# A two-layer decoder step on one core: samples' products, scores and weighted values placed anew, and accumulators that are not zeroed

## The chip, the cores and the metric

One NeuronCore of a Trainium2 chip. The metric is the device time of one execution in microseconds. Engines are named as in the profile: PE is TensorE's matmuls (PEld its weight loads), DVE VectorE, ACT ScalarE, POOL GpSimd, SP the engine that issues most of the DMAs.

## The reference

One inference step of a decoder trunk with two layers of model width 1024, for a prompt of 1024 tokens and 8 samples of one token each, which share all weights:

```python
def a_mixer(hn, w_in, lb, hg_gain, mem_k, mem_v, w_o, s0):     # layer 0
    q_h, f_h, i_h, g_h, q_m = jnp.split(hn @ w_in, 5, axis=-1)
    ...
    o, S = hgrn2_scan(q, k, v, logf, s0)       # S = f*S + k v ; o = q S, per head 128x128
    o = rmsnorm(o.astype(hn.dtype), hg_gain) * jax.nn.silu(g_h).reshape(...)
    om = mem_attend(q_m.reshape(B, L, MEM_HEADS, MEM_DH), mem_k, mem_v)
    out = jnp.concatenate([o.reshape(B, L, MIX_HALF), om.reshape(B, L, MIX_HALF)], axis=-1) @ w_o

def b_mixer(hn, w_in, bias, k_all, v_all, q_pos, k_pos, mem_k, mem_v, w_o):   # layer 1
    q_s, q_m = jnp.split(hn @ w_in, 2, axis=-1)
    os_ = stick_breaking(...)                  # over the shared K/V, with a running sum of log(1-p)
    om = mem_attend(...)                       # 4 heads over 256 memory tokens

# every layer: h = h + rmsnorm(mix); h = h + rmsnorm(swiglu(rmsnorm(h)))
```

For each sample the memory attention and the stick-breaking attention run over that sample's own cache: 256 keys and values of 4 heads x 128.

## The kernel before, in words

The 1024 prompt tokens are two groups, g = 0 and g = 1, of 512; the 8 samples ride with group 1, which is then 520 wide. Every weight product keeps float32 accuracy by splitting both operands into a high and a low part in the matmul's reduced format, and takes three matmuls. A weight piece of 512 x 128 is loaded by SP into `wraw` (5 buffers); ACT casts it to the high part (L217, or L611 for the gate products) into `ws` (5 buffers), and DVE subtracts to get the low part (L218, L613). `split[0]` always names the last of these subtractions. Activations are split alike (L238, L239).

A part of a layer is a generator that yields after each piece of work. `weave((generator, weight), ...)` draws from several of them in turn, in the ratio of their weights, and so writes one program in which the parts are interleaved; the framework's scheduler then sets the order on each engine. `tc.issue_after(ins)` ties what is issued inside it behind an instruction. The places that matter here:

- `a1` is layer 0's mixer for group 1. `a1.core` (380 to 497 us) is the prompt's recurrence. `a1.sample` (until about 550 us) is the samples' recurrence, `hgrn_sample`: for each of four heads DVE decays the state (L1329), makes the new term (L1330) from values that a DMA reads from `vd`, adds it (L1331) and multiplies with the queries (L1335). State and term are tiles of a pool `C()` of four 128x1024 buffers.
- `a1.mem` and `a1.mem_sample` (550 to 750 us) are its memory attention, for the prompt and for the samples. For a sample, `sample_scores` loads the keys into a `C()` tile and the query row `qd` (broadcast by DMA to all partitions), multiplies (L1097) and sums (L1100) on DVE. A softmax over 256 keys follows (L1169 to L1178). `sample_pv` loads the values, multiplies all of them by their probabilities (L1120, one 128x1024 product on DVE), adds the two halves of keys (L1123), splits the sum (L238, L239), and PE adds over the partitions with selector matmuls (L1111).
- `b1` is layer 1's mixer for group 1 (1500 to 1890 us): `b1.sb` (`sb_prompt`) is the prompt's stick-breaking, woven with the samples' own (`sb_sample`, its cache read by indirect DMAs on POOL) and with their memory attention, both by the two functions above. In `sb_prompt` a step makes scores (PE L1588), a bias and a cap (DVE L1599 to L1603), a softplus (ACT L1574, L1575), a running sum and a difference (DVE L1608, L1610), an exponential (ACT L1611), transposes (PE L1617, copied by ACT L1619), and the products with the values (PE L1628), which add over a head's steps in one PSUM bank. DVE sets that bank to zero first (L1625).
- Beside them run the feed-forward parts (`f0.part`, `rest()`: matmuls L231, L544, L618; ACT L261 to L263, L561; DVE L260, L264, L859), the matmuls that keep PE busy.

PSUM: `S()` has three banks, `NS()` one; the other four hold products. ACT's exponential and its sigmoid-like functions need different tables; a change of table shows as ACT_TABLE_LOAD.

Of the kernel before, what the change touches and what calls it, by code (L numbers as in the profile page):

```python
# [13 lines left out]
AF = mybir.ActivationFunctionType  # L14
ALU = mybir.AluOpType
# [8 lines left out]
def tile_decoder(  # L24
# [96 lines left out]
    def S():  # L121
        return smp.tile([P, 512], F32, tag="s", name=nm("s"))
# [39 lines left out]
    def gcol(l, i, k):  # L162
        o = (l * 4 + i) * ND + k
        return par[:, o : o + 1]
# [253 lines left out]

    def residual(g, R, rstd, gc, store, acc=None, first=False):
        n = NG[g]  # L420
        w = D // 2 if first else n
        ht = [xpool.tile([P, 2, w], F32, tag=f"x{g}", name=nm("ht")) for _ in range(ND // 2)]
        for j in range(ND // 2):
            if first:
                t0 = g * G + j * P
                nc.sync.dma_start(ht[j].rearrange("p a n -> p (a n)"), x_prompt[0, t0 : t0 + P, :])
            else:
                nc.sync.dma_start(ht[j], hs[g][:, 2 * j : 2 * j + 2, :n])
        for k in range(ND):
            if first:  # L430
                ps = NS()
                for tb in range(CH):
                    xf = ht[tb].rearrange("p a n -> p (a n)")
                    nc.tensor.transpose(ps[:, tb * P : (tb + 1) * P], xf[:, k * P : (k + 1) * P], ident)
            nc.vector.scalar_tensor_tensor(R[k][:, :n], R[k][:, :n], gc(k), rstd[:, :n], op0=ALU.mult, op1=ALU.mult)
            if first:
                nc.vector.tensor_add(R[k][:, :G], R[k][:, :G], ps)
                if g:
                    nc.vector.tensor_add(R[k][:, G:n], R[k][:, G:n], xsraw[:, k, :])
            else:  # L440
                nc.vector.tensor_add(R[k][:, :n], R[k][:, :n], ht[k // 2][:, k % 2, :])
# [16 lines left out]
    class out_proj:  # L458
# [35 lines left out]
        def finish(self):  # L494
            g, l = self.g, self.l
            rstd = rstd_from(self.acc, NG[g], 1.0 / D)
            acc = small([P, WID], tag="st", bufs=3)
            yield from residual(g, self.R, rstd, lambda k: gcol(l, 1, k), not self.last, acc, l == 0)
            r2 = rstd_from(acc, NG[g], 1.0 / D)
            yield  # L500
            yield from normed(g, self.R, r2, lambda k: gcol(l, 2, k), self.x, self.last)
# [575 lines left out]
    def sample_scores(q, load, sc):  # L1077
        qc = small([P, H * NB], tag="ss")
        for i in range(2):
            nc.vector.tensor_copy(  # L1080
                qc[:, i * 2 * NB : (i + 1) * 2 * NB].rearrange("p (h b) -> p h b", h=2), q[i][:, :, G : G + NB]
            )
        pq = S()
        for h in range(H):
# [20 lines left out]
    def sample_pv(pT, load, xo, k0):  # L1105
# [10 lines left out]
        for b in range(NB):  # L1116
            vt = load(b)
            v4 = vt.rearrange("p k (h d) -> p k h d", h=H)
            with tc.issue_after(split[0].ins):
                nc.vector.tensor_mul(v4, v4, pv4[:, :, :, b].unsqueeze(3).to_broadcast([P, 2, H, P]))  # L1120
            yield
# [10 lines left out]
        yield  # L1132
        pr = S()
        for h in range(H):
# [29 lines left out]
    def mem_attn_sample(l, qm, xo):  # L1164
# [3 lines left out]
        yield  # L1168
        pr = S()  # L1169
        for blk in range(2):  # L1170
# [8 lines left out]
        yield  # L1179
        pb = S()  # L1180
        for blk in range(2):
# [3 lines left out]
        yield  # L1185
        yield from sample_pv(pT, mem_loader(cache_mem_v, l), xo, H)

# [107 lines left out]
    def hgrn_sample(Ft, Kt, Qt, vd):  # L1295
# [25 lines left out]
        for h in range(H):  # L1321
# [6 lines left out]
            with tc.issue_after(split[0].ins):  # L1328
                nc.vector.tensor_mul(stv, stv, col(Ft))  # L1329
            nc.vector.tensor_mul(vbv, vbv, col(Kt))  # L1330
            nc.vector.tensor_add(st, st, vb)  # L1331
            nc.sync.dma_start(st_sample[0, :, h].rearrange("b k v -> k b v"), stv)
            total()
            yield
            nc.vector.tensor_mul(vbv, stv, col(Qt))  # L1335
            for a in range(2):
# [129 lines left out]
    class mixer_a:  # L1466
# [49 lines left out]
        def mem_sample(self):  # L1516
            yield from mem_attn_sample(0, self.Qm, self.xo)

# [58 lines left out]
    def sb_prompt(g, Qs, xo):  # L1577
# [44 lines left out]
        def values(h, vh, i, wt, spans):  # L1622
            if i == 0:
                po[0] = S()
                nc.vector.memset(po[0], 0.0)  # L1625
            for c, s, a, w in spans:
                for o in range(0, w, P):
                    nc.tensor.matmul(  # L1628
                        po[0][:, c * P : (c + 1) * P], vh[:, s, o : o + P], wt[:, a + o : a + o + P],
                        start=False, stop=(s == 0 and o == w - P), skip_group_check=True,  # L1630
                    )

            if i == len(units) - 1:
                put(xo, h, slice(0, G), po[0])

        po, asked, turned = [None], None, None

# [19 lines left out]
    def sb_sample(Qs, xo):  # L1657
# [7 lines left out]
        yield  # L1665
        cu = S()
        nc.tensor.matmul(cu[:, 0:HB], trif, e[:, 0:HB], start=True, stop=False)
# [7 lines left out]
    class mixer_b:  # L1675
# [33 lines left out]
        def mem_sample(self):  # L1709
            yield from mem_attn_sample(1, self.Qm, self.xo)  # L1710

# [110 lines left out]
    f0 = ffn(0, 0, o0.x)  # L1822
    weave((a1.core(), 22), (f0.part(0), 14), (islice(w0, 16), 17))
    a1.open()
    weave((a1.sample(), 12), (a1.gate(), 4), (f0.part(1), 14), (w0, 9))

# [7 lines left out]

    weave((chain(a1.merge(), a1.mem()), 27), (a1.mem_sample(), 82), (rest(), 33))
    xk0, xb0 = [], []
# [83 lines left out]
```

## Time and profile before

| | |
|---|---|
| time, three runs | 2412.99, 2409.97, 2412.3 us (median 2412.3) |
| the profiled execution | 2411.39 us, its span 2409.7 us, mean granted clock 0.998 |
| DVE products L1120, the weighted values | 24 of 1.22 us, 29.3 us |
| DVE products and sums of the samples' scores, L1097 and L1100 | 24 of 1.22 us and 24 of 1.21 us |
| DVE memsets L1625 | 8 of 0.485 us, 3.9 us |
| DMAs of the samples' memory keys | 16 of 512 KB, median 3.6 us from issue to landing |

A row of a group names the line, the engine and the operation, what is written and read, how often, and then the busy time in all, the mean of one in ns, and the idle time of the engine just before them with what ended it. A row of the waits says which engine and line waited for which, how long in all, how many times and the longest. A row of the timeline has the start, the length, the instruction and, in brackets, the idle time before it and what ended that.

### The profile page before, as it was taken

Reading aid. Unit: us, or ns where it says so; the run is one execution under the profiler, and the core shown is the slowest. Engines: PE = TensorE matmul, PEld = TensorE weight load, DVE = VectorE, ACT = ScalarE, POOL = GpSimd, SP = SyncE. Lnnn points to the kernel's source line nnn. Section 1 sums busy time; section 2 is a strip of 40 time slices with the busy share of each in tenths; the row PEclk is TensorE's granted clock in tenths of the full one; section 3 lists DMA queues with packets and bytes.
Section 4 is the critical chain, followed back from the end, with each engine's and each line's share of the span. In section 5 each row is a group of like instructions: output and inputs, shape, how many; then the busy total and the mean of one; then the engine's idle time right before and its main releaser. Section 6 shows DMA issues by size and latency. Waiting matters only on the chain.

```text
span 2409.7 us, 42324 instructions
## 1 busy us (share of the span) xinstructions
PE 2381.2 (99%) x15962; PEld 2158.6 (90%) x15962; DVE 1738.1 (72%) x3227; ACT 1275.5 (53%) x2548; POOL 113.2 (5%) x187
## 2 busy tenths in 40 slices
PE   9999999999999999999999999999999999999998
PEld 7888989888789998999999989887778899999998
DVE  5867558666896676878665777778787679676866
ACT  4547544444454554667544554556454566554445
POOL 1001202101000000000001200111000000000000
PEclk9999999999999999999999999999999999999999
DMA  6454766577644447332568846545344354343342
GB/s 195 119 169 118 171 193 167 123 191 182 200 136 141 145 144 219 115 110 81 170 177 217 229 145 189 166 140 154 113 153 122 97 158 136 105 130 100 111 127 76
DMA packets 514639, 357.59 MB, mean 148 GB/s; under 512 B 20173, under 2 KB 463674, under 8 KB 514434
## 3 DMA queue, kind: packets, MB, share of 16 engines
q1 hardware_dynamic: 498562, 312.93, 43.8%
q0 software_dynamic: 15872, 41.95, 7.4%
q8 instruction: 126, 2.06, 0.4%
q14 instruction: 79, 0.65, 0.1%
HBM read 322.86 MB, written 65.49 MB: 161 GB/s over the span
## 4 chain that ended last, share of the span: by engine, by line
PE 50%; DVE 2%; ACT 2%; issue 1%; DMA 1%; DVEq 0%; SPq 0%; ACTq 0%
PE mm L231 17%; PE q L618 16%; PE q L790 10%; PE q L544 1%; PE s L1628 1%; PE q L822 1%; PE s L1588 1%; PE s L1050 1%; PE s L1031 1%; PE s L1617 1%; DMA b<-qd 0%; DVE x L239 0%; PE ns L1111 0%; DVE ws L218 0%; PE s L1018 0%
## 5 line engine op out<-in xcount | busy, mean ns | idle before, releaser
L231 PE MATMUL mm<-x,ws 128*128 128x512 f32 (+1 forms) x5016 | 926.9, 342 | 5.5 <-DVE ws L218 2.5
L231 PEld LDWEIGHTS mm<-x,ws 128*128 128x128 f32 x5016 | 776.1, 189 | 116.0 <-DVE ws L218 3.2
L217 ACT CAST ws<-w 128x512 fp32r<-128x512 f32 x596 | 347.5, 585 | 432.6 <-PE mm L231 269.0
L218 DVE TENSOR_TENSOR ws<-w,ws 128x512 fp32r<-128x512 f32 x596 | 380.9, 645 | 227.7 <-ACT ws L217 225.1
L790 PE MATMUL q<-m,ws 128*128 128x260 f32 (+1 forms) x2496 | 304.5, 283 | 0.4
L790 PEld LDWEIGHTS q<-m,ws 128*128 128x128 f32 x2496 | 300.1, 189 | 1.6 <-ACT m L238 0.7
L618 PE MATMUL q<-y,ws 128*128 128x260 f32 (+1 forms) x1920 | 249.7, 284 | 0.2 <-ACT q L626 0.2
L618 PEld LDWEIGHTS q<-y,ws 128*128 128x128 f32 x1920 | 237.7, 189 | 1.5 <-ACT q L630 0.6
L618 PE MATMUL q<-x,ws 128*128 128x260 f32 (+1 forms) x1668 | 220.4, 283 | 3.0 <-ACT ws L611 1.6
L618 PEld LDWEIGHTS q<-x,ws 128*128 128x128 f32 x1668 | 207.9, 189 | 4.4 <-ACT ws L611 2.2
L231 PE MATMUL mm<-m,ws 128*128 128x512 f32 x768 | 187.2, 398 | 0.0
L611 ACT CAST ws<-w 128x512 fp32r<-128x512 f32 x206 | 125.1, 619 | 97.7 <-PE q L790 30.7
L613 DVE TENSOR_TENSOR ws<-w,ws 128x512 fp32r<-128x512 f32 x206 | 139.4, 688 | 45.1 <-ACT ws L611 43.0
L231 PEld LDWEIGHTS mm<-m,ws 128*128 128x128 f32 x768 | 142.7, 188 | 31.1
L799 DVE TENSOR_TENSOR r<-r,q 128x260 f32<-128x260 f32 (+1 forms) x160 | 60.6, 420 | 46.2 <-PE q L790 45.9
L544 PE MATMUL q<-x,ws 128*128 128x260 f32 (+1 forms) x720 | 87.1, 282 | 0.0
L544 PEld LDWEIGHTS q<-x,ws 128*128 128x128 f32 x720 | 86.4, 189 | 0.2
L238 ACT CAST m<-t 128x512 fp32r<-128x512 f32 (+1 forms) x88 | 54.8, 622 | 49.3 <-DVE t L859 26.7
L611 ACT CAST ws<-b 128x512 fp32r<-128x512 f32 x82 | 50.6, 620 | 38.8 <-PE q L790 13.4
L613 DVE TENSOR_TENSOR ws<-b,ws 128x512 fp32r<-128x512 f32 x82 | 56.4, 688 | 17.8 <-ACT ws L611 17.5
L239 DVE TENSOR_TENSOR m<-t,m 128x512 fp32r<-128x512 f32 (+1 forms) x88 | 60.7, 690 | 11.2 <-ACT m L238 10.4
L290 DVE TENSOR_TENSOR st<-st,n 128x512 f32<-128x512 f32 (+1 forms) x91 | 62.2, 691 | 4.2 <-ACT n L289 3.0
(422 smaller groups left out, 3092.6 us busy)
## 6 DMA issues: line engine op xcount, KB each, us to landing
w<-in_w_gu SPq DMA_DIRECT2D x275, 256.0 KB, 3.3
w<-in_w_down SPq DMA_DIRECT2D x160, 256.0 KB, 3.2
wsum<-in_w_gu POOLq DMA_DIRECT2D x48, 512.0 KB, 6.4
w<-in_w_in_a SPq DMA_DIRECT2D x80, 256.0 KB, 3.0
w<-in_w_o SPq DMA_DIRECT2D x64, 256.0 KB, 2.8
w<-wsum SPq DMA_DIRECT2D x61, 256.0 KB, 3.1
b<-in_w_gu SPq DMA_DIRECT2D x39, 256.0 KB, 4.3
b<-wsum SPq DMA_DIRECT2D x39, 256.0 KB, 3.4
```

The costliest lines, as they stand in the source:

```text
L217: nc.scalar.copy(ws[:, 0, :n, :], raw[:, :n, :])
L218: split[0] = nc.vector.tensor_sub(ws[:, 1, :n, :], raw[:, :n, :], ws[:, 0, :n, :].bitcast(F32))
L231: nc.tensor.matmul(ps[:, a, : PW[g]], wt, xt[k][:, xi, o : o + PW[g]], start=(k == 0 and wi == 0), stop=(k == nk - 1 and wi == 2),)
L238: nc.scalar.copy(dst[0], src)
L239: nc.vector.tensor_sub(dst[1], src, dst[0].bitcast(F32))
L290: nc.vector.tensor_add(acc[:, :n], acc[:, :n], t[:, :n])
L544: ins = nc.tensor.matmul(pp[a][:, :h], wt, xt[k][:, xi, a * h : (a + 1) * h], start=(k == 0 and wi == 0), stop=(k == ND - 1 and wi == 2),)
L611: nc.scalar.copy(w[:, 0, :], src)
L613: split[0] = nc.vector.tensor_sub(w[:, 1, :], src, w[:, 0, :].bitcast(F32))
L618: nc.tensor.matmul(ps[:, :h], w[:, wj, k * P : (k + 1) * P], x[:, xi, :], start=(first and k == 0 and wi == 0), stop=(k == 3 and wi == 2), ...
L790: nc.tensor.matmul(pp[a][:, :h], wt, mids[k][:, xi, a * h : (a + 1) * h], start=(k == 0 and wi == 0), stop=(k == nf - 1 and wi == 2),)
L799: nc.vector.tensor_add(d, d, pp[a][:, :h])
```

## The change

1. The samples' recurrence gets a yield between the decay and the new term, and both the new term and the product with the queries are issued behind `split[0]`.
2. The first nine steps of `a1.mem_sample` (the query rows and the scores of four samples) are woven into `a1.core`; weights of the weaves change.
3. `sb_prompt` no longer zeroes its bank: the first matmul of a head starts it, the others are tied behind that one.
4. Four transposes and a sum of the samples go from `S()` to `NS()`.
5. The residual of layer 1, group 0, is issued behind `split[0]`.
6. The samples' weighted values are made by ACT: eight copies of 128x128, each with the probability as a scale read from a pointer, in place of one DVE product.

```diff
-    def residual(g, R, rstd, gc, store, acc=None, first=False):
+    def residual(g, R, rstd, gc, store, acc=None, first=False, paced=False):
...
-            nc.vector.scalar_tensor_tensor(R[k][:, :n], R[k][:, :n], gc(k), rstd[:, :n], op0=ALU.mult, op1=ALU.mult)
+            with tc.issue_after(split[0].ins) if paced else nullcontext():
+                nc.vector.scalar_tensor_tensor(R[k][:, :n], R[k][:, :n], gc(k), rstd[:, :n], op0=ALU.mult, op1=ALU.mult)
...
-            yield from residual(g, self.R, rstd, lambda k: gcol(l, 1, k), not self.last, acc, l == 0)
+            yield from residual(g, self.R, rstd, lambda k: gcol(l, 1, k), not self.last, acc, l == 0, l == 1 and g == 0)
...
-        pq = S()
+        pq = NS()
...
-            with tc.issue_after(split[0].ins):
-                nc.vector.tensor_mul(v4, v4, pv4[:, :, :, b].unsqueeze(3).to_broadcast([P, 2, H, P]))
+            for k in range(2):
+                for h in range(H):
+                    with tc.issue_after(split[0].ins):
+                        nc.scalar.activation(v4[:, k, h, :], v4[:, k, h, :], AF.Copy, scale=pv4[:, k, h, b : b + 1])
...
-            nc.vector.tensor_mul(vbv, vbv, col(Kt))
+            yield
+            with tc.issue_after(split[0].ins):
+                nc.vector.tensor_mul(vbv, vbv, col(Kt))
...
-            nc.vector.tensor_mul(vbv, stv, col(Qt))
+            with tc.issue_after(split[0].ins):
+                nc.vector.tensor_mul(vbv, stv, col(Qt))
...
-                po[0] = S()
-                nc.vector.memset(po[0], 0.0)
+                po[0], po[1] = S(), None
             for c, s, a, w in spans:
                 for o in range(0, w, P):
...
+                    with tc.issue_after(po[1].ins) if po[1] else nullcontext():
+                        m = nc.tensor.matmul(
+                            po[0][:, c * P : (c + 1) * P], vh[:, s, o : o + P], wt[:, a + o : a + o + P],
+                            start=po[1] is None, stop=(s == 0 and o == w - P), skip_group_check=True,
+                        )
+                    po[1] = po[1] or m
...
-        cu = S()
+        cu = NS()
...
-    weave((a1.core(), 22), (f0.part(0), 14), (islice(w0, 16), 17))
+    ms = a1.mem_sample()
+    weave((a1.core(), 22), (f0.part(0), 14), (islice(ms, 9), 9), (islice(w0, 16), 17))
     a1.open()
-    weave((a1.sample(), 12), (a1.gate(), 4), (f0.part(1), 14), (w0, 9))
+    weave((a1.sample(), 16), (a1.gate(), 4), (f0.part(1), 14), (w0, 9))
...
-    weave((chain(a1.merge(), a1.mem()), 27), (a1.mem_sample(), 82), (rest(), 33))
+    weave((chain(a1.merge(), a1.mem()), 36), (ms, 74), (rest(), 33))
```

`mem_attn_sample` also asks for its output `xo` by a lambda, since that does not exist yet when its first steps run. Lines of the changed kernel stand up to 8 lower.

How this stands in the order of the engines, at three places. First DVE in the samples' recurrence, before, at the second head; `c` are the pool's tiles, `ws` weight pieces, and L1330 of `c_5465` is the new term of the third head:

```order
L1335 TENSOR_TENSOR c_5206<-c_5205,a_2690 128x1024
L218 TENSOR_TENSOR ws_5378<-w_5376,ws_5378 128x512
L264 TENSOR_TENSOR a_5209<-a_5209,t_5269 128x520
L239 TENSOR_TENSOR b_5415<-c_5206,b_5414 128x512
L239 TENSOR_TENSOR b_5419<-c_5206,b_5418 128x512
L260 TENSOR_SCALAR t_5310<-mm_5285 128x512
L218 TENSOR_TENSOR ws_5424<-w_5422,ws_5424 128x512
L264 TENSOR_TENSOR t_5311<-t_5311,t_5310 128x512
L218 TENSOR_TENSOR ws_5429<-w_5427,ws_5429 128x512
L1329 TENSOR_TENSOR c_5360<-c_5360,a_2291 128x1024
L1330 TENSOR_TENSOR c_5465<-c_5465,a_2493 128x1024
L859 TENSOR_TENSOR t_5311<-t_5311,mm_5330 128x512
```

The same engine in the changed kernel, from behind the second head's sum to the third head's new term (L1335 is now the new term, L1341 the product with the queries):

```order
L218 TENSOR_TENSOR ws_5625<-w_5623,ws_5625 128x512
L264 TENSOR_TENSOR a_5246<-a_5246,t_5306 128x520
L239 TENSOR_TENSOR m_5495<-t_5444,m_5495 128x512
L218 TENSOR_TENSOR ws_5630<-w_5628,ws_5630 128x512
L1341 TENSOR_TENSOR c_5359<-c_5358,a_2690 128x1024
L260 TENSOR_SCALAR t_5565<-mm_5516 128x520
L239 TENSOR_TENSOR b_5664<-c_5359,b_5663 128x512
L218 TENSOR_TENSOR ws_5673<-w_5671,ws_5673 128x512
L264 TENSOR_TENSOR a_5246<-a_5246,t_5565 128x520
L218 TENSOR_TENSOR ws_5678<-w_5676,ws_5678 128x512
L1332 TENSOR_TENSOR c_5501<-c_5501,a_2492 128x1024
L1335 TENSOR_TENSOR c_5502<-c_5502,a_2493 128x1024
```

Before, the third head's new term stood behind the second head's decay; now it stands behind its own. The last use of the buffer that the third head's values are loaded into (L239 of the first head) stood 6 instructions ahead of it, and now stands 26 ahead.

Second, ACT at the end of layer 0's memory attention, before: `x_5204` is the last piece of the attention's output and `ws_7548` the first weights of the gate product to follow it:

```order
L238 CAST m_7505<-t_7356 128x512
L1023 COPY b_7524<-s_7519 128x512
L238 CAST x_5201<-s_7529 128x8
L238 CAST x_5202<-s_7529 128x8
L238 CAST x_5203<-s_7529 128x8
L238 CAST x_5204<-s_7526 128x512
L238 CAST x_5204<-s_7529 128x8
L611 CAST ws_7548<-b_7546 128x512
```

And in the changed kernel, where `x_5241` is that last piece and `ws_7608` those first weights:

```order
L217 CAST ws_7458<-w_7456 128x512
L238 CAST x_5241<-ns_7280 128x8
L238 CAST a_7397<-b_7398 128x256
L238 CAST a_7395<-b_7400 128x256
L562 ACTIVATE t_7293<-q_7304 128x256
L562 ACTIVATE t_7293<-q_7305 128x256
L217 CAST ws_7530<-w_7528 128x512
L238 CAST a_7395<-b_7404 128x256
L238 CAST a_7396<-b_7402 128x256
L217 CAST ws_7535<-w_7533 128x512
L238 CAST a_7397<-b_7509 128x256
L612 CAST ws_7608<-b_7606 128x512
```

The attention's last casts stood directly ahead of the gate's weights; now other casts stand between.

Third, ACT where the weighted values of the first samples are made in the changed kernel (L1123 are the copies with a scale, `n` the split of their sum); before, none of the L1123 rows stood here:

```order
L1123 ACTIVATE c_6554<-c_6554,ss_6532 128x128 x8
L1123 ACTIVATE c_6630<-c_6630,ss_6532 128x128 x3
L238 CAST n_6604<-c_6554 128x512
L1123 ACTIVATE c_6630<-c_6630,ss_6532 128x128
L238 CAST m_6600<-t_6513 128x512
L1062 ACTIVATE b_6614,sme_6613<-s_6608,nmx_6611 128x256 x2
L1024 COPY b_6625<-s_6620 128x512
L1123 ACTIVATE c_6630<-c_6630,ss_6532 128x128 x4
L217 CAST ws_6729<-w_6727 128x512
L217 CAST ws_6802<-w_6800 128x512
L238 CAST n_6683<-c_6630 128x512
L1123 ACTIVATE c_6712<-c_6712,ss_6532 128x128 x8
```

Eight copies of a sample stand in a row or are broken by other work, and weight casts (L217) come behind them.

More of the change, by code (lines that the diff above doesn't have):

```diff
@@ L1 @@
-from contextlib import ExitStack
+from contextlib import ExitStack, nullcontext
 from itertools import islice
@@ L1132, in sample_pv @@
         yield
-        pr = S()
+        pr = NS()
         for h in range(H):
@@ L1168, in mem_attn_sample @@
         yield
-        pr = S()
+        pr = NS()
         for blk in range(2):
@@ L1179, in mem_attn_sample @@
         yield
-        pb = S()
+        pb = NS()
         for blk in range(2):
@@ L1185, in mem_attn_sample @@
         yield
-        yield from sample_pv(pT, mem_loader(cache_mem_v, l), xo, H)
+        yield from sample_pv(pT, mem_loader(cache_mem_v, l), xo(), H)
     carry = const.tile([P, H, P], F32, name="carry")
@@ L1516, in mem_sample @@
         def mem_sample(self):
-            yield from mem_attn_sample(0, self.Qm, self.xo)
+            yield from mem_attn_sample(0, self.Qm, lambda: self.xo)
     def kv_proj(g, xt):
@@ L1623, in values @@
             if i == 0:
-                po[0] = S()
-                nc.vector.memset(po[0], 0.0)
+                po[0], po[1] = S(), None
             for c, s, a, w in spans:
                 for o in range(0, w, P):
[L1628 to L1631, printed above, removed]
+                    with tc.issue_after(po[1].ins) if po[1] else nullcontext():
[4 more added lines that the diff above has]
+                    po[1] = po[1] or m
             if i == len(units) - 1:
                 put(xo, h, slice(0, G), po[0])
-        po, asked, turned = [None], None, None
+        po, asked, turned = [None, None], None, None
         def step(new=None):
@@ L1709, in mem_sample @@
         def mem_sample(self):
-            yield from mem_attn_sample(1, self.Qm, self.xo)
+            yield from mem_attn_sample(1, self.Qm, lambda: self.xo)
     def store_y(g, R):
```

## The prediction

> **What bounds the kernel now.** I read the page first, for which engine is full.
>
> ```profile
> span 2409.7 us, 42324 instructions
> PE 2381.2 (99%) x15962; PEld 2158.6 (90%) x15962; DVE 1738.1 (72%) x3227; ACT 1275.5 (53%) x2548; POOL 113.2 (5%) x187
> ```
>
> TensorE (PE) is busy for 2381.2 of 2409.7 us, so all its idle time is 28.5 us. The change leaves TensorE the same 15,315 matmuls and their shapes; nothing can be gained except out of the idle time, and VectorE (DVE) and ScalarE (ACT) matter only where TensorE comes to stand behind them. The profiled execution took 2411.39 us, 1.7 us more than its span; it lies 0.9 us under the median of the runs (2412.3). I sum against 2411.4.
>
> Then the busy times by stretch (columns: stretch, length, PE, PEld, DVE, ACT, POOL, granted clock, DMA share, GB/s), for the stretches where the change moves work.
>
> ```profile
> 380.00:500.00 120.00, 120.00 (x695) 101.71 (x694) 79.35 (x194) 50.73 (x104) 16.73 (x33) 1.00 0.59 143
> 560.00:640.00 80.00, 78.24 (x375) 63.85 (x374) 53.89 (x86) 33.35 (x63) 3.67 (x6) 0.98 0.62 175
> 640.00:695.00 55.00, 55.00 (x253) 44.26 (x252) 48.89 (x82) 25.95 (x59) 0.00 (x0) 1.00 0.57 172
> 695.00:750.00 55.00, 53.43 (x398) 49.48 (x397) 46.28 (x106) 35.21 (x75) 0.00 (x0) 1.00 0.39 116
> 1622.00:1706.00 84.00, 84.00 (x403) 66.28 (x402) 66.23 (x100) 48.70 (x91) 10.04 (x8) 1.00 0.45 136
> 1812.00:1890.00 78.00, 78.00 (x359) 63.13 (x358) 56.38 (x99) 37.42 (x84) 0.00 (x0) 1.00 0.37 111
> 377.00:760.00 383.00, 377.84 (x2128) 320.81 (x2127) 279.28 (x538) 179.33 (x359) 26.85 (x51) 1.00 0.62 166
> 1500.00:1900.00 400.00, 395.28 (x1989) 320.98 (x1989) 311.58 (x497) 211.02 (x412) 28.04 (x24) 1.00 0.45 137
> ```
>
> Over the two long touched stretches (last rows) TensorE idles 383 − 377.84 = 5.2 and 400 − 395.28 = 4.7 us. **9.9 us is the most that the change can bring there.** The rest is which instruction ends each gap.
>
> **The change part by part.**
>
> *A, no zeroed banks.* Eight memsets (L1625) leave VectorE, and the first L1628 matmul of a head starts its bank itself. Two of the eight cost TensorE time. The timeline at those places (start, length, engine):
>
> ```profile
> 1552.44 0.74 DVE L1603 TENSOR_SCALAR b<-s,biasp 128x512 f32<-128x512 f32 x1
> 1553.29 0.48 DVE L1625 MEMSET s<- 128x512 f32 x1
> 1553.87 0.80 PE L1628 MATMUL s<-b,a 128*128 128x128 f32 x5 [1.49 <-issue]
> 1752.45 0.48 DVE L1625 MEMSET s<- 128x512 f32 x1
> 1753.04 0.80 PE L1628 MATMUL s<-b,a 128*128 128x128 f32 x5 [1.40 <-issue]
> ```
>
> TensorE starts 0.1 us after each memset ends (1553.29 + 0.48 = 1553.77), having idled 1.49 and 1.40 us: the profile calls it "issue", but the memset stood behind other VectorE work, and its end is what let the matmul go. The matmul's other inputs were made a step earlier. Gain 2.9 us; at least 0, if the next input is just as late, at most 2.9.
>
> *B, the recurrence of the samples.* Today VectorE comes to L1330 before its data, and everything behind it waits:
>
> ```profile
> DVE c L1330 <- DMA c<-vd: 11.1, 3, 3.9
> c<-vd SPq DMA_DIRECT2D x4, 512.0 KB, 5.7
> 525.56 1.23 DVE L1330 TENSOR_TENSOR c<-c,a 128x1024 f32<-128x1024 f32 x1 [3.52 <-DMA c<-vd]
> 522.79 3.17 PE L231 MATMUL mm<-x,ws 128*128 128x512 f32 x13
> 527.53 0.70 PE L231 MATMUL mm<-x,ws 128*128 128x512 f32 x2 [1.56 <-DVE t L859]
> ```
>
> VectorE waited 3.52 us; L859, next in its order, came late, and TensorE idled 1.56 us for that. The new yield puts each head's Kt product behind its own decay and not behind the decay of the head before: in the order of VectorE the gap from the last use of a buffer to the product that wants the new data in it grows from 5 or 6 instructions to 23 or 26. At the 0.68 us of an ordinary one that is 3.4 us before and 15.6 us now, against transfers that land in 5.7 us. Nothing is late next on this path but the ordinary weight subtractions. Gain 1.6 us, bounds 0 and 1.6. Only one of the three waits reached TensorE by so much.
>
> *C, half of the scores moved into the recurrence's core.* Around 633 us VectorE does scores without one weight subtraction (L218) between:
>
> ```profile
> 631.18 1.22 DVE L1097 TENSOR_TENSOR c<-c,b 128x1024 f32<-128x1024 f32 x1
> 632.31 0.69 DVE L239 TENSOR_TENSOR m<-t,m 128x512 fp32r<-128x512 f32 x1
> 632.91 1.22 DVE L1100 TENSOR_REDUCE sc<-c 128x8 f32<-128x1024 f32 x1
> 634.04 1.22 DVE L1097 TENSOR_TENSOR c<-c,b 128x1024 f32<-128x1024 f32 x1
> 635.18 0.68 DVE L218 TENSOR_TENSOR ws<-w,ws 128x512 fp32r<-128x512 f32 x1
> 635.92 1.30 PE L231 MATMUL mm<-x,ws 128*128 128x512 f32 x3 [1.76 <-DVE ws L218]
> ```
>
> TensorE idles 1.76 us until that L218 is done. Four of eight samples' scores (a product and a reduction each) leave this place; the other four still pile up in it, between fewer yields. I take half, 0.9 us; bounds 0 and 1.8. They go to 380 to 500 us, where TensorE never idles. There VectorE takes 4 × (1.22 + 1.21) = 9.7 us more, 89.1 of 120 us, 74%: room that hides them. Their transfers come too, four k loads and four rows of qd, into a stretch where the DMA engines are busy for 0.59. What queues behind a scores product that waits for its row is a weight subtraction. The rows for this wait today, in the whole program:
>
> ```profile
> DVE c L1097 <- DMA b<-qd: 11.5, 9, 2.6
> b<-qd SPq DMA_DIRECT2D x24, 256.0 KB, 4.3
> ```
>
> Nine waits in 24 products, none over 2.6 us, against a lead of five weight buffers (priced in E). Cost of this step 0, bounds 0 and 2.6.
>
> *D, the memory attention ends earlier.* Today ScalarE reaches the first weights of the gate product (L611) behind the small casts of the attention:
>
> ```profile
> 744.14 0.66 ACT L238 CAST x<-s 128x512 fp32r<-128x512 f32 x2 [0.34 <-PE s L1031]
> 744.68 0.63 ACT L611 CAST ws<-b 128x512 fp32r<-128x512 f32 x1
> 745.36 0.50 PE L618 MATMUL q<-x,ws 128*128 128x256 f32 x2 [1.26 <-ACT ws L611]
> 746.17 1.11 PE L618 MATMUL q<-x,ws 128*128 128x256 f32 x7 [0.31 <-DVE ws L613]
> ```
>
> TensorE idles 1.26 + 0.31 = 1.6 us. With the new weights (36, 74, 33) the attention's last casts stand well ahead of L611 in ScalarE's order, with other products between. Gain 1.6, bounds 0 and 1.6.
>
> *E, the weighted values on ScalarE.* This is the step that can cost. VectorE loses 24 products, ScalarE gains 24 × 8 = 192 copies of 128x128 with a scale from a pointer. The trace has no such copy. The nearest groups (count, busy us, mean ns of one):
>
> ```profile
> L1120 DVE TENSOR_TENSOR c<-c,ss 128x1024 f32<-128x1024 f32 x16 | 19.6, 1222 | 4.6 <-DMA c<-in_cache_mem_v 4.6
> L1384 ACT COPY b<-a 128x128 f32<-128x128 f32 x16 | 4.3, 308 | 3.7 <-DVE a L1379 3.7
> L1378 ACT COPY b<-a 128x256 f32<-128x256 f32 x16 | 5.9, 400 | 0.6 <-DVE a L264 0.6
> L832 ACT ACTIVATE r<-r,par 128x256 f32<-128x256 f32 x8 | 3.8, 503 | 0.1
> 745.72 1.15 ACT L611 CAST ws<-b 128x512 fp32r<-128x512 f32 x2
> L561 ACT ACT_TABLE_LOAD x4 | 5.1, 1283 | 0.1
> ```
>
> At 256 elements the pointer scale adds 503 − 400 = 0.10 us, so one copy of 128 lasts about 0.31 + 0.10 = 0.41 us. Two casts back to back take 1.15 us and not 2 × 0.62, so 0.09 is shared: 0.32 us of engine time each, 2.5 us a sample where VectorE took 1.22. Lower bound 0.31 − 0.09 = 0.22, upper 0.50 (the row at twice the width): 1.8 to 4.0 us a sample, 192 copies 42 to 96 us, 61 at my value.
>
> The Trainium skill, ScalarE: Activation LUTs, section "Rules for kernel authors", says to do a multiplication on VectorE and not on ScalarE. The rows above agree on the price, twice the time, but price on an engine is not time of the kernel; by the rule the change would lose, and it is the slower rival below. The same page's section "What ACT_TABLE_LOAD costs" gives 186 ns + 0.833 ns an element + 93 ns a pointer, less 93 ns back to back; I estimate 0.29 us from it, 56 us in all.
>
> Does ScalarE have room? Between 640 and 750 us it is busy 25.95 + 35.21 = 61.2 us; 64 copies add 20.5, and four table loads (two before the exponentials, two at L561) go with 5.1: 76.6 of 110, 70%. In 1622 to 1706 it comes to 48.70 + 20.5 = 69.2 of 84, 82%; in 1812 to 1890 to 57.9 of 78, 74%. VectorE falls there to 66.2 − 9.8 = 56.4 of 84. So there is room on average, but in lumps: eight copies that stand in a row hold a weight cast (L217) up for 2.5 us, sometimes eleven do, for 3.5. A weight tile feeds 12 matmuls of 128x512, some 2.9 us (13 take 3.17 in B's rows), and five tiles can lie ready, which covers one lump and mostly two. The waits for the v loads (4.6 us in 5 waits today) go to ScalarE too, 0.9 us each, again with weight casts behind them. The nearest row of a lump on one engine is that of C: 1.76 us lost to 4 us without a subtraction. Over 24 lumps I take one such loss, **+1.8 us**; lower bound 0 (or a gain, since VectorE is freed of 29 us where exponential chains wait for it: L1608 and L1610), upper bound 24 × (2.5 − 1.2) = 31 if every lump lay on the path in full.
>
> *F, the rest.* The tied residual rows of layer 1 change no row of VectorE's order there, and so cost and bring nothing. The transposes that go to the other single bank wait for data that they wait for anyway; I put 0, bounds ±0.5.
>
> **Sum.** 2.9 + 1.6 + 0.9 + 1.6 = 7.0 us of gain, 1.8 of loss: 2411.4 − 5.2 = **2406.2 us**.
>
> **Rivals.**
>
> *R1, slower: ScalarE becomes late.* The place is the last 16 samples, 1620 to 1890 us, where the stick-breaking chain (L1574, L1575, L1611, L1619) runs on ScalarE through the copies, and the 8 of 640 to 750. What speaks for it: 82% in the mean, and chains that already wait long between engines:
>
> ```profile
> ACT b L1611 <- DVE b L1610: 33.5, 29, 2.4
> DVE b L1608 <- ACT b L1575: 19.9, 25, 1.7
> ```
>
> Against it: TensorE idles nothing in 1622 to 1706 and 1812 to 1890 now, with VectorE at 79% in the first. If half of the 1.3 us that a lump is longer than the product comes through in each of 24, it costs 15.6 us: 2411.4 − 7.0 + 15.6 = 2420.0. It eats the gain from 0.3 us lost a lump (24 × 0.3 = 7.2), and the kernel is slower beyond the measurement from 0.5 (24 × 0.5 = 12); a copy nearer to 0.5 than to 0.32 us would do that.
>
> *R2, about the same: the waits move.* The DVE wait of B returns at another product, the attention's tail of D is replaced by a queue of copies, C's pile stays. Then A alone holds, against E: 2411.4 − 2.9 + 1.8 = 2410.3. For it speaks that only 1.5 us sits at each place and any other late input may end it; against it, that each gap has one named releaser.
>
> *R3, more: VectorE with 33 us less work (29 of products, 3.9 of memsets) lets every gap of the touched stretches close.* 2411.4 − 9.9 = 2401.5.
>
> **How the numbers follow.** My forecast 0.36, R1 0.20, R2 0.32, R3 0.12. A measurement of this kernel tells about 0.2% from no change, 4.8 us: faster means under 2407.5, slower over 2417.1. Forecast and R3 are faster, 0.48; R2 is the same, 0.32; R1 slower, 0.20. The range reaches from 2397 (R3, and 4 us that shorter spacing of the matmuls might add) to 2420 (R1's price); beyond it lie R1's worse half and little else.
>
> **What would show it.** A: no idle over 1 us ahead of the first values matmul of any head. B: VectorE's wait for vd gone from the list of waits, none of 1.5 us near 525. C: the gap near 633 halved. D: no wait of L618 on L611 at its start. E: the copies near 0.41 us each, few PE waits on weight casts (L217) in the three stretches; if these show idle over 5 us, I am wrong by R1. If TensorE idle in the two stretches stays near 9.9 us, R2 holds.

## The result, and the profile after

The changed kernel takes 2406.07 us in the median of 16 runs (2404.33 to 2409.98), the kernel before 2412.03 us beside it (16 runs, 2409.4 to 2415.14). The ratio is 0.9977, with a 95% interval of 0.9970 to 0.9984: 5.5 us less, between 3.9 and 7.2. The forecast was 2406.2 us.

The page of the changed kernel, its span and its engines:

```profile
span 2404.4 us, 42487 instructions
PE 2377.7 (99%) x15962; PEld 2156.4 (90%) x15962; DVE 1710.3 (71%) x3195; ACT 1322.5 (55%) x2736; POOL 113.7 (5%) x187
```

VectorE has 28 us less to do and ScalarE 47 us more; TensorE's idle time went from 28.5 to 26.7 us, and its busy time down by 3.5, though its work is the same; 1.7 us of these 3.5 are explained below the next table. The busy times of the same long stretches (columns as in the prediction; the program is 5 us shorter, so they hold slightly more of what follows):

```profile
377.00:760.00 383.00, 382.50 (x2191) 327.14 (x2190) 274.82 (x537) 195.89 (x425) 28.80 (x51) 1.00 0.63 168
1500.00:1900.00 400.00, 394.12 (x1983) 320.01 (x1981) 292.42 (x479) 244.19 (x542) 26.72 (x24) 1.00 0.45 135
```

Read them against those of before: in the first stretch TensorE's idle time fell from 5.2 to 0.5 us. In the second it rose from 4.7 to 5.9 us, although two waits of 1.4 us on the memsets are gone from it. In this execution the change won in layer 0 and lost a little in layer 1.

Both programs have the same number of matmuls, so the start of the n-th can be compared. The table has, for the kernels of this study, by how much each stretch became longer or shorter against the profiled run of the kernel before (us; the borders are where the orders of work agree; A to F are the parts of the prediction):

| stretch of before | changed | changed, VectorE products | A alone | B alone | C and D alone | B, C and D |
|---|---|---|---|---|---|---|
| 0 to 376 | −0.9 | −0.3 | −0.9 | +0.3 | +0.5 | −0.9 |
| 376 to 560 | −2.3 | −2.3 | −0.7 | −2.3 | +4.7 | −2.3 |
| 560 to 760 | −5.1 | −4.1 | −0.6 | −1.5 | −5.0 | −4.7 |
| 760 to 1490 | +1.5 | −0.3 | 0.0 | −0.3 | +0.1 | −0.1 |
| 1490 to 1900 | +1.1 | −1.7 | 0.0 | +0.7 | +1.8 | +0.3 |

Cells where a kernel changes nothing tell how far single executions differ: up to 1.5 us. The +1.5 between 760 and 1490 is such a cell: one wait of 1.7 us at 1349 us on work that the change does not touch, which no other run has.

Part of the difference is the granted clock. In the profiled run of the kernel before it is 0.50 from 636.4 to 639.8 us, just behind the wait of 1.76 us there. The stretch (columns as before):

```profile
632.00:640.00 8.00, 6.24 (x21) 4.66 (x20) 8.00 (x11) 3.01 (x5) 0.00 (x0) 0.79 0.72 226
```

3.4 us at half clock are some 1.7 us of work lost (an estimate, half of the length), and they stand in every cell of the row 560 to 760, since all are taken against that execution. Without them the changed kernel is 3.4 us shorter there and not 5.1. A alone has such a stretch at 743 us, B alone at 1551 us, C and D alone at 494 and at 1555 us; the other three kernels of the table have none.

### The profile page after: what moved, and what is told of

Read it like the earlier page. It is cut to its first block, busy times and chain, and to the rows that moved or that the text cites. A ratio compares the mean times of both kernels' runs of the same rounds, so it can differ in the third digit from the quotient of the medians.

```text
span 2404.4 us, 42487 instructions
## 1 busy us (share of the span) xinstructions
PE 2377.7 (99%) x15962; PEld 2156.4 (90%) x15962; DVE 1710.3 (71%) x3195; ACT 1322.5 (55%) x2736; POOL 113.7 (5%) x187
## 4 chain that ended last, share of the span: by engine, by line
PE 85%; DVE 6%; ACT 4%; DMA 3%; issue 2%; SPq 0%; DVEq 0%; ACTq 0%
PE mm L231 37%; PE q L619 18%; PE q L791 11%; PE q L545 4%; PE mm L1235 2%; PE s L1414 1%; DMA b<-qd 1%; PE s L1051 1%; PE s L1032 1%; PE mm L968 1%; PE mm L995 1%; PE q L823 1%; DVE ws L218 1%; ACT c L1123 1%; DVE b L1614 1%
## 5 line engine op out<-in xcount | busy, mean ns | idle before, releaser
L217 ACT CAST ws<-w 128x512 fp32r<-128x512 f32 x596 | 346.6, 584 | 396.1 <-PE mm L231 228.4
L239 DVE TENSOR_TENSOR m<-t,m 128x512 fp32r<-128x512 f32 (+1 forms) x88 | 60.9, 691 | 13.5 <-ACT m L238 12.5
```

The lines of the kernel that those rows point to most:

```text
L217: nc.scalar.copy(ws[:, 0, :n, :], raw[:, :n, :])
L239: nc.vector.tensor_sub(dst[1], src, dst[0].bitcast(F32))
```

## Experiments

All times are medians beside runs of the kernel before on the same chip (2409.9 to 2410.3 us there). The changed kernel's own ratio, 0.9977, was taken where the kernel before took 2412.03 us, so the ratios carry the comparison, and not the times.

**VectorE's products in place of the copies.** The changed kernel, with

```diff
-            for k in range(2):
-                for h in range(H):
-                    with tc.issue_after(split[0].ins):
-                        nc.scalar.activation(v4[:, k, h, :], v4[:, k, h, :], AF.Copy, scale=pv4[:, k, h, b : b + 1])
+            with tc.issue_after(split[0].ins):
+                nc.vector.tensor_mul(v4, v4, pv4[:, :, :, b].unsqueeze(3).to_broadcast([P, 2, H, P]))
```

> The changed kernel with the weighted values made by VectorE again (24 products of 1.22 us), all else kept. Theory: the copies cost something in layer 1's mixer for group 1, where TensorE lost 1.1 us from 1490 to 1900 us although both memset waits (2.9 us) are gone, so 4 us were lost anew there; if the copies did it, this kernel takes about 2402 us, with fewer waits of the transposes (L1623) on the exponential (L1617). Rival: the new waits come from the other reordering (values matmuls directly behind the transposes, score products ahead of the chain) and the copies cost nothing: 2406 us, the waits still there. My prediction's own term was 1.8 us: 2404.

Measured: 2404.19 us, ratio 0.9975 (0.9965 to 0.9984), against 0.9977 of the changed kernel. The timed difference is 0.5 us, within the intervals of about 2 us: the theory of 4 us falls. The waits of the transposes on the exponential are partly there without the copies, too (3.7 us in 4 waits between 1490 and 1900 us, 5.9 in 6 with them, 1.8 in 3 in the kernel before), so of the 4.1 us of new waiting 1.9 have another cause than the copies.

**The copies alone.** The kernel before, with the same edit the other way round.

> The kernel before with nothing changed but the weighted values, made by 192 ScalarE copies. Theory: 4 us lost at most, 2416 us; the prediction's term: 2414; rival (copies cost nothing, or VectorE's freedom brings a little): 2411 to 2412. ScalarE busy time should rise by some 60 us whichever is true.

Measured: 2410.7 us, ratio 1.0005 (0.9996 to 1.0014): 1.2 us more, between 1.0 less and 3.4 more. ScalarE's busy time rose from 1275.5 to 1328.1 us, 52.6 us, and VectorE's fell by 23.9. The prediction's 1.8 us lies in the interval, and so does no loss at all; 4 us does not.

**The copies twice.** The changed kernel, each sample's eight copies followed by eight with a scale of one.

> The changed kernel with every copy done twice (the second with a scale of one), 384 copies, 16 in a row for a sample, 4.7 us of ScalarE a sample. If lumps on ScalarE reach TensorE in proportion (theory, 4 us for 24 lumps of 2.4 us), the doubled lumps cost 4 us more at the least and, past the lead of the weight buffers, rather 10: 2410 to 2416 us. Rival (lumps are covered): under 2408 us.

Measured: 2416.79 us, ratio 1.0026 (1.0015 to 1.0037), 0.0049 or 11.8 us above the changed kernel. So lumps on ScalarE can reach TensorE, and past the lead of the weight tiles they do. The timeline of this kernel at one of the lumps, where L1127 are the added copies:

```profile
664.08 1.89 ACT L1123 ACTIVATE c<-c,ss 128x128 f32<-128x128 f32 x6
665.84 2.46 ACT L1127 ACTIVATE c<-c,ones 128x128 f32<-128x128 f32 x8
668.18 0.63 ACT L217 CAST ws<-w 128x512 fp32r<-128x512 f32 x1
668.86 2.37 PE L231 MATMUL mm<-x,ws 128*128 128x512 f32 x6 [2.18 <-ACT ws L217]
```

Fourteen copies hold a weight cast up from 664.1 to 668.2 us, and TensorE idles 2.18 us for it. In the whole of this kernel TensorE waits six times for L217, 6.8 us; in the changed kernel, with half the copies, not once. Those waits are 6.8 of the 11.8 us; the rest was not traced to a place. The first eight copies of a sample cost 0.5 us in all, with an interval that holds 0 and 3, and the second eight some 12: the price is not in proportion to the number of copies, and rises somewhere between 2.4 and 4.7 us of ScalarE a sample.

**Half and half.** Four copies on ScalarE and one 128x512 product on VectorE for each sample.

> The changed kernel with half of each sample's weighted values on ScalarE (4 copies, 1.2 us) and half on VectorE (one 128x512 product, 0.68 us). Theory: between the changed kernel and the one with VectorE alone, 2404 us; rival: 2406 us, no difference.

Measured: 2405.71 us, ratio 0.9976 (0.9967 to 0.9985). The same as with all (0.9977) or none (0.9975) within the intervals: the division of this work between the two engines does not show in the time.

**The memsets back.** The changed kernel with the old `values`, L1625 included.

> The changed kernel with the eight memsets and the old values matmuls back, the copies and all else kept. By the prediction 2.9 us come back: 2409 us against 2406, with TensorE idle of 1.4 us twice ahead of the first values matmul. Rival (what the memset's absence gains at 1552 and 1751 us is lost again at the next transposes, which wait for the exponential: the changed kernel shows such waits of 1.3, 1.1 and 0.8 us that the kernel before has not): within 1 us of the changed kernel, 2405 to 2407.

Measured: 2405.14 us, ratio 0.9982 (0.9973 to 0.9991), 1.2 us above the changed kernel's, but with an uncertainty of some 2.7 us from the two intervals, so that neither 0 nor 2.9 is excluded. The traces show where the waits went. A row of the waits of TensorE between 1490 and 1900 us says who waited for what, how long in all, how often and the longest; first the kernel before, then the changed kernel:

```profile
PE s L1628 <- issue: 2.9, 2, 1.5
PE s L1617 <- ACT b L1611: 1.8, 3, 1.1
```

```profile
PE s L1623 <- ACT b L1617: 5.9, 6, 1.7
```

With the memsets back in the changed kernel TensorE waits 2.5 us for them again, twice, and only 1.9 us (4 times) for the exponential, where the changed kernel waits 5.9: what the memsets take at one place is not waited for at the next.

**No memsets, alone.** The kernel before with

```diff
-                po[0] = S()
-                nc.vector.memset(po[0], 0.0)
+                po[0], po[1] = S(), None
```

and the tied matmuls of the change.

> The kernel before with the memsets alone removed (the first values matmul of a head starts its bank). Prediction: 2.9 us less than before, both idle times of 1.4 us gone. Rival: 0 to 1 us less, with new waits of the transposes on the exponential between 1540 and 1620 us.

Measured: 2409.19 us, ratio 0.9992 (0.9983 to 1.0001): 1.9 us less, between 4.1 less and 0.2 more. The trace shows what becomes of the gain. The two waits at the memsets are gone, and TensorE comes to the transposes that much sooner. There it waits for the exponential. First this kernel's TensorE, then its VectorE ahead of that wait:

```profile
1598.22 1.02 PE L1588 MATMUL s<-a,a 128*128 128x512 f32 x2
1600.99 0.66 PE L1617 MATMUL s<-ident,b 128*128 128x128 f32 x4 [1.75 <-ACT b L1611]
```

```profile
1590.00 0.28 DVE L218 TENSOR_TENSOR ws<-w,ws 128x128 fp32r<-128x128 f32 x1
1591.64 1.23 DVE L1097 TENSOR_TENSOR c<-c,b 128x1024 f32<-128x1024 f32 x1 [1.36 <-DMA b<-qd]
1592.90 1.22 DVE L1100 TENSOR_REDUCE sc<-c 128x8 f32<-128x1024 f32 x1
1594.04 0.68 DVE L260 TENSOR_SCALAR t<-mm 128x512 f32<-128x512 f32 x1
1594.64 0.68 DVE L218 TENSOR_TENSOR ws<-w,ws 128x512 fp32r<-128x512 f32 x1
1595.24 0.34 DVE L1601 SCALAR_TENSOR_TENSOR b<-s,biasp,cap 128x128 f32<-128x128 f32 x1
```

The chain from the scores to the exponential begins on VectorE at L1601. That stands behind a sample's product and sum, which first waited 1.36 us for a query row. In the kernel before VectorE has the same order there and waits for the row, too (0.98 us), but TensorE does not wait:

```profile
1601.27 1.02 PE L1588 MATMUL s<-a,a 128*128 128x512 f32 x2
1601.56 0.63 ACT L1611 ACTIVATE b<-b 128x512 f32<-128x512 f32 x1 [1.88 <-DVE b L1610]
1602.24 0.66 PE L1617 MATMUL s<-ident,b 128*128 128x128 f32 x4
```

The exponential ended at 1601.56 + 0.63 = 1602.19 us and the transposes began at 1602.24: it came only just in time. Without the memsets TensorE is ready for the transposes 3.05 us sooner than before, and the exponential 1.25 us sooner. Between 1490 and 1900 us the waits of TensorE on the exponential grew from 1.8 us (3) to 4.7 us (4), which is the 2.9 us of the two memset waits again. In the time 1.9 us of gain are left, with an interval that holds both 0 and 2.9.

**The recurrence alone.** The kernel before with the yield, the two ties and the weight 16.

> The kernel before with the samples' recurrence alone changed (a yield, two ties, the weight 16). Prediction: 1.6 us less, up to 2.1 with the small gap at 545 us; no wait of VectorE for vd. Rival (the wait moves to a later product): no difference, a wait for vd still in the list.

Measured: 2408.2 us, ratio 0.9994 (0.9985 to 1.0003): 1.4 us less, an interval that still holds no change. The trace is clearer: no wait for vd is left, the stretch from 376 to 560 us is 2.3 us shorter, and TensorE runs through the place of the old gap:

```profile
516.63 12.63 PE L231 MATMUL mm<-x,ws 128*128 128x512 f32 x54
```

**The early scores alone.** The kernel before with the query transposes in the other bank, and

```diff
-    weave((a1.core(), 22), (f0.part(0), 14), (islice(w0, 16), 17))
+    ms = a1.mem_sample()
+    weave((a1.core(), 22), (f0.part(0), 14), (islice(ms, 9), 9), (islice(w0, 16), 17))
...
-    weave((chain(a1.merge(), a1.mem()), 27), (a1.mem_sample(), 82), (rest(), 33))
+    weave((chain(a1.merge(), a1.mem()), 36), (ms, 74), (rest(), 33))
```

> The kernel before with the early scores alone (nine steps in the core, the weights 36, 74, 33, the query transposes in the other bank). Prediction: C and D together, 2.5 us less. The changed kernel's trace has 5.1 us less between 560 and 760 us; if that is this part's own doing, 5 us less; if the copies did part of it by freeing VectorE, 3.5 to 4 us less.

Measured: 2411.99 us, ratio 1.0006 (0.9997 to 1.0015). No gain at all, and none of the three expectations. From 560 to 760 us it is 5.0 us shorter, as hoped, 1.7 of them the low clock of the kernel before; from 376 to 560 it is 4.7 us longer. The place, in this kernel:

```profile
491.73 1.22 DVE L1330 TENSOR_TENSOR c<-c,a 128x1024 f32<-128x1024 f32 x1 [4.75 <-DMA c<-vd]
492.87 0.68 DVE L239 TENSOR_TENSOR n<-b,n 128x512 fp32r<-128x512 f32 x1
493.61 0.61 PE L279 MATMUL s<-n,onesr 128*128 128x512 f32 x1 [2.73 <-DVE n L239]
```

The keys of the early scores occupy buffers of the pool that `vd` is loaded into: the load of `vd` for the first head is issued at 484.93 us, just when the fourth sample's sum (L1100) has ended at 484.90; in the kernel before that head's new term was made at 377 us already. The untied new term (L1330) stands in VectorE's order ahead of its data, VectorE waits 4.75 us, and a norm (L239, L279) behind it stops TensorE for 2.73 us. The granted clock of 0.50 from 493.9 us on accounts for some 1.7 us more of the 4.7.

**The recurrence and the early scores together.**

> The kernel before with the recurrence's part and the early scores together, neither copies nor the memsets' part. Alone the early scores lost 4.6 us at 490 us (VectorE came to the first head's new term L1330 and waited 4.75 us for vd, with the weight subtractions and a norm behind it) and gained 5 us from 560 to 760. Theory: the two parts depend on each other, the yield and the tie take that product out of the way; the sum of the parts as the traces show them, 2.3 + 5.0 = 7.3 us less than before, no idle of TensorE over 1 us from 377 to 560 us. Rival (the parts only add): -1.4 + 0 to 2 = about 1 us less than before.

Measured: 2406.05 us, ratio 0.9986 (0.9977 to 0.9995): 3.4 us less, between 1.2 and 5.5. The sum of the two alone is −1.4 + 1.4 = 0; together they bring 3.4 us more, and the three intervals make that uncertain by nearly 4, so the times alone do not settle it. The 7.3 us of the theory lie outside the interval. The trace is clearer: the 4.7 us lost near 490 are gone from it, and no idle of TensorE over 1 us is left from 377 to 560 us. So the recurrence's part is what lets the scores move; its yield, ties and weight were not tried one by one. The profiled run, a quick one of its kernel, is 7.1 us shorter than that of before. Of this 0.9 lie ahead of the first change and some 1.7 are the low clock of the kernel before; the 4.5 us that are left agree with the times.

**The query rows one sample ahead**, three times: with VectorE's products, with the memsets' part alone, and in the changed kernel itself.

```diff
-            qb = B()
-            nc.sync.dma_start(qb, qd[b].partition_broadcast(P))
+            qb = ahead
+            if b < NB - 1:
+                ahead = B()
+                nc.sync.dma_start(ahead, qd[b + 1].partition_broadcast(P))
```

> The changed kernel with VectorE's products, and the query rows of a sample loaded one sample ahead (one more 128x512 buffer in use). Theory: without the memsets TensorE reaches the transposes sooner, and there the VectorE chain is late, which waits for query rows (up to 1.4 us, then 2.4 us of score work ahead of the chain). With the rows ahead, that chain is sooner: some 2 us less than the kernel with VectorE's products alone, ratio to before 0.9967. Rival (the chain is late for its own length): no difference, ratio 0.9975, TensorE still waiting over 1.5 us at 1593 and 1777 us. The buffer taken away may cost by itself.

> The kernel before without memsets, with the query rows one sample ahead. Theory: the waits of the transposes at 1598 and 1783 us (2.1 and 2.3 us) shrink and the memsets' full 2.9 us comes out, 0.9988 or less of before. Rival: the same as without memsets alone (0.9992), the two waits unchanged.

> The changed kernel as it is (copies on ScalarE) with the query rows one sample ahead. Theory: some 2 us less than the changed kernel, ratio to before 0.9969; rival: no difference, 0.9977.

Measured: 2407.56 us, ratio 0.9992 (0.9983 to 1.0001); 2411.5 us, ratio 1.0005 (0.9996 to 1.0014); 2408.7 us, ratio 0.9994 (0.9985 to 1.0003). Each is 3 to 4 us more than the same kernel without the edit (0.9975, 0.9992, 0.9977). It did not do what it was meant to: VectorE's waits for query rows came to 10.5 us where they were 8.9 (VectorE's products) and to 11.8 where they were 10.2 (no memsets). Of the two waits on the exponential that it was to shorten, the one near 1600 us did shrink, from 1.41 to 0.66 us and from 1.75 to 0.55, but the one near 1783 us grew, from 1.39 to 2.04 and from 1.89 to 2.31. What was added is one more held buffer of seven, and with it TensorE waits for the exponential oftener between 1490 and 1900 us: 7 times where it was 4, 8 where it was 4, 8 where it was 6. These waits in all grew by no more than 1.4 us, so most of the loss lies elsewhere; in the two kernels with the moved scores 1.9 us of it lie between 376 and 560 us. So whether the late query rows are what makes the chain late is not settled by it, and the fix is no fix. That the buffer is the cause of the loss is argued, not shown.

## Why the prediction came out

The total was right to 0.1 us (2406.2 foretold, 2406.07 measured; as a gain 5.2 against 5.5, with an interval from 3.9 to 7.2). Its terms were not all right: A was too large, C and D were too small, and the two errors cancelled. That the total is so close is luck.

The premise that nothing can be gained except out of idle time left out the clock: in the profiled runs TensorE's idle time fell by 1.8 us and its busy time by 3.5, and some 1.7 of these are the stretch at half clock in the kernel before. Two small slips in the working change nothing: the traces count 15,962 matmuls in both kernels, transposes among them, where the working has 15,315, and a loss of 12 us in R1 gives 2416.4, still under the 2417.1 from which the prediction calls a kernel slower.

**A, the memsets: too large.** Put at 2.9 us. Alone it measured 1.9 us (−0.2 to 4.1), taken back 1.2 us, and by its trace between 1490 and 1900 us nothing. Beside the other parts the traces of that stretch disagree: with VectorE's products it is 1.9 us shorter than with B, C and D alone, and with the copies 1.7 us longer than with the memsets back. So where the waits go is shown, and how much of the 2.9 us is left is not. The step that failed is "at least 0, if the next input is just as late" with the choice of the upper end: the next input *was* nearly as late. The prediction looked only at what else the values matmul waits for, not at the transposes one step on, whose exponential ended 0.05 us before they began. The test that it named (no idle over 1 us ahead of a values matmul) came out as foretold and did not catch this.

**B, the recurrence: right.** 1.6 us foretold, 2.3 us in the trace (1.8 of them idle time), 1.4 measured with an interval that reaches past both. VectorE's waits for vd (11.1 us) went from the list.

**C and D, the scores and the attention's end: too small, and with a condition not seen.** Put at 0.9 + 1.6 us. From 560 to 760 us the changed kernel is 5.1 us shorter, 3.4 without the low clock of the kernel before; the two waits there, 1.76 and 1.57 us, make 3.3. The two were not run apart. The place near 633 us runs through,

```profile
631.73 4.31 PE L231 MATMUL mm<-x,ws 128*128 128x512 f32 x18
```

so all 1.76 us came out and not half. The low clock at that place belongs to the one execution: it was 1.00 there in the other runs that have this wait (1.2 to 1.7 us long). D came out: 737.44 is the start of the gate product, without a wait.

```profile
737.44 1.59 PE L619 MATMUL q<-x,ws 128*128 128x256 f32 x12
```

The price of moving the scores into the core was put at 0, since VectorE has room there. That holds only together with B. Alone the move costs 4.7 us in the core (2.7 of waiting, some 1.7 of low clock behind it), not by VectorE's time but by a buffer and an order; the prediction counted the load and the DMAs and did not count whose buffers the keys would hold.

**E, the copies: the price of one right, the loss not resolved.** Put at 1.8 us of loss. The times give 1.2 us alone and 0.5 in the changed kernel, and both intervals hold 0 and 1.8. The price of one copy was good:

```profile
L1123 ACT ACTIVATE c<-c,ss 128x128 f32<-128x128 f32 x128 | 40.9, 395 | 11.4 <-DMA c<-in_cache_mem_v 11.1 <-DVE ws L218 0.2
L1123 ACT ACTIVATE c<-c,sc 128x128 f32<-128x128 f32 x64 | 21.6, 393 | 2.7 <-DMA c<-in_cache_sb_v,pidx 2.7
```

0.395 us where 0.41 was put; 62.5 us in all, where 61 was put. ScalarE's busy time, in which an overlap counts once, is 52.3 us more than with VectorE's products. Six in a row take 1.87 us (row at 1655.42 below), (1.87 − 0.39) / 5 = 0.30 us each, against 0.32. By the formula of the Trainium skill, ScalarE: Activation LUTs, section "What ACT_TABLE_LOAD costs", the estimate for such an instruction is 0.386 us, and 0.293 us back to back. The trace agrees (0.395 and 0.30). The rule of the Trainium skill, ScalarE: Activation LUTs, section "Rules for kernel authors", multiplication on VectorE, is right about the engine's time (2.4 us a sample against 1.22) and decided nothing here: ratio 0.9975 with VectorE, 0.9977 with ScalarE. One loss of the size that was put in (1.8 us) can be pointed at. ScalarE waits for a page of values, then the lump and the casts behind it make the softplus late, and so the exponential:

```profile
1655.42 1.87 ACT L1123 ACTIVATE c<-c,sc 128x128 f32<-128x128 f32 x6 [1.74 <-DMA c<-in_cache_sb_v,pidx]
...
1661.08 0.63 ACT L1581 ACTIVATE b<-b 128x512 f32<-128x512 f32 x1
1661.74 1.27 DVE L1614 TENSOR_TENSOR_SCAN b<-b 128x128 f32<-128x128 f32 x2 [0.23 <-ACT b L1581]
1663.05 0.69 DVE L1616 TENSOR_TENSOR b<-b,b 128x512 f32<-128x512 f32 x1
1663.78 0.63 ACT L1617 ACTIVATE b<-b 128x512 f32<-128x512 f32 x1 [1.27 <-DVE b L1616]
1664.46 0.66 PE L1623 MATMUL s<-ident,b 128*128 128x128 f32 x4 [1.73 <-ACT b L1617]
```

With VectorE's products the same transposes start without a wait, and with the copies alone on the kernel before they wait 1.23 us:

```profile
1661.08 1.02 PE L1592 MATMUL s<-a,a 128*128 128x512 f32 x2
1661.93 0.60 PE L1621 MATMUL s<-ident,b 128*128 128x128 f32 x4
```

```profile
1668.69 0.66 PE L1619 MATMUL s<-ident,b 128*128 128x128 f32 x4 [1.23 <-ACT b L1613]
```

At this place every profiled kernel that has the copies in the size of the change waits, and none with VectorE's products: 1.73 us in the changed kernel, 1.23 with the copies alone, 0.94 with the memsets back, 1.46 with the rows ahead. With half the copies the wait is as long, 1.79 us, and ScalarE's wait for the page still stands in it (1.31 us). So the length of the lump alone does not set this loss; what the wait for the page has in it was not tested apart. Against it, a wait of 1.58 us on the softmax at 695 us (L1068, on VectorE) in the kernel with VectorE's products is 0.51 in the changed one. Other kernels with the moved scores and without the copies wait 0.6 to 1.1 us there, so a saving of 1 us by the copies is not shown. It was not a weight cast that came late, as the prediction had it, but the softplus; the casts come late only with lumps twice as long.

**F, the rest**, was put at 0 and never run alone: the tied residual and the transposes of the softmax in the other bank are in the changed kernel and in those made from it.

**The rivals.** R1 (ScalarE late) fell at this size; with twice the copies its mechanism, waits on weight casts, is there. R2 (the waits move) holds for A alone. R3 did not come: the idle time of the two long stretches went from 9.9 to 6.4 us and not to none, and with the copies alone VectorE is 23.9 us freer and the time no shorter.

## What to carry to other kernels

A wait that one row names is worth its length only if nothing else on the next step is ready just as late; follow the waiting engine one step further and read how early its next input is. Moving work into a stretch with room also takes buffers there: look at who else draws from the pool, and at which product stands untied ahead of its data. On an engine that is half idle a lump of work can be nearly free, as eight copies a sample were here, and twice the lump dear, as sixteen were: count how much of the work behind it lies ready.

## What was not expected of the hardware

The granted clock falls to 0.50 for 3.4 us behind some waits of TensorE. Leaving out the first 40 us and the end of each run, the fourteen traces have nine such stretches, and each begins 0.2 to 1.9 us after a wait has ended. All five waits of TensorE that were longer than 2.1 us are followed by one; of the 42 between 1.2 and 2.1 us only four are, the one at 636 us in the kernel before among them. Why these four and not the others stays open. So in these runs a long wait could cost some 1.7 us beyond its length (an estimate, half of 3.4), but did not each time.

Executions of one kernel differ by some 5.7 us between slowest and quickest (2409.4 to 2415.14 us in 16 runs of the kernel before, 2404.33 to 2409.98 in 16 of the changed one), so a difference of 2 us needed ten runs and the trace together, and in several cases stayed unclear even so.
